# Spreading a column of token values over the free axis: a PE transpose in place of a float32 product with the identity

## The chip, the cores and the metric

The kernel runs on one core of one Trainium2 chip. The metric is the device time of one execution in microseconds, lower is better. TensorE (PE) multiplies matrices, VectorE (DVE) and ScalarE (ACT) do elementwise work, GpSimd (POOL) the small powers, and SyncE's queue (SP) issues the loads.

## The reference, cut to what matters

Two transformer-like blocks run over 256 tokens of width 1024: a first one (gated feed-forward layers, forgetting attention, a gated delta rule, cross attention to a memory) and a second of depth 2 (feed-forward layers, a convolution and a state-space mixer, a gated projection). Between the layers stands, again and again, a norm over the width of each token:

```python
def rms_norm(x, gain):
    xf = x.astype(jnp.float32)
    y = xf * lax.rsqrt(jnp.mean(xf * xf, axis=-1, keepdims=True) + EPS)
    return (y * gain.astype(jnp.float32)).astype(x.dtype)

def l2_norm(x):
    return x * lax.rsqrt(jnp.sum(x * x, axis=-1, keepdims=True) + EPS)

def swiglu(x, w_gate, w_up, w_down):
    return (jax.nn.silu(x @ w_gate) * (x @ w_up)) @ w_down
...
def first_block(...):
    f = swiglu(rms_norm(h, ffn1_pre_norm[l]), ffn1_w_gate[l], ffn1_w_up[l], ffn1_w_down[l])
    h = h + FFN_RESIDUAL_WEIGHT * rms_norm(f, ffn1_post_norm[l])
    mixed = hybrid_mixer(rms_norm(h, mix_pre_norm[l]), ...)
    h = h + rms_norm(mixed @ w_out[l], mix_post_norm[l])
    ...
```

Everything is float32.

## The kernel before

Activations lie transposed: eight tiles of 128 features (partitions) by 256 tokens (free axis). Every weight is loaded in units of up to 128x1024, split by ACT into a rounded high half `hi` (line 299) and by DVE into the remainder `lo` (line 300), and each product of weight and activation is three matmuls of 128x256 (`mm3`: high by high, high by low, low by high), all through `mm` on line 267. `raw` has four buffers, `hi` and `lo` three each, so that a new unit waits until PE is done with the one three before it. PSUM tiles are `pm` (projections) and `px` (everything else).

A norm goes like this. The squares of the tiles are added up (`acc`), and PE sums them over the partitions, with the two halves of the tokens as stationary operands and a column of ones moving: the result has the 128 tokens of a half on the partitions, one column for each half. DVE adds the epsilon (`rv`, line 419), POOL raises it to the power -0.5 (`rs`, line 421). To multiply the activations, which have the tokens on the free axis, the column must be spread: every partition must hold the whole row of token values. That is `spread`: for each half `t`, the column, repeated 128 times along the free axis by a step of zero, is the stationary operand of a product with the identity. `rstd_b` copies the result out to `rb`; `post` and the group norm of `mixer2` read it in PSUM. The `l2_norm` values of the gated delta rule go the same way (`rk` and, with the output norm, `of`), and `mixer1` spreads a copy of its column, `mrt`.

`transpose` (line 270) is PE's transpose by the same identity; the kernel uses it elsewhere, for the chunks of the two mixers and the attention weights.

The order of work on each engine is not written out: a scheduler takes the program's operations by priority and by its own estimates of when each can start and how long it takes. `high_priority(-n)` puts an operation n places later; `late` and `APART` do so for sums and spreads, so that other products stand between the two halves of a sum or of a spread and cover the way over DVE and POOL.

Of the kernel before, what the change touches and what calls it, by code (L numbers as in the profile page):

```python
# [15 lines left out]
P = 128  # L16
# [121 lines left out]
class Net:  # L138
# [285 lines left out]
    def spread(self, r, cols=(0, 1), apart=0):  # L424

        ps = self.bank()
        for t in range(2):
            j = cols[t]
            with self.tc.high_priority(-apart * t):
                self.mm(ps[:, t * P:(t + 1) * P], r[:, j:j + 1].to_broadcast([P, P]), self.ident)  # L430
        return ps[:, :S]

    def rstd_b(self, acc, n, mult=1.0):
# [1066 lines left out]
```

## Time and profile before

| | |
|---|---|
| timed runs, median of 3 | 2211.42 us (2211.13 to 2215.14) |
| the profiled execution's own time | 2205.73 us |
| its span, first to last instruction | 2203.9 us |
| PE busy | 2171.3 us, 99% |
| DVE busy | 1553.1 us, 70% |
| ACT busy | 1191.8 us, 54% |
| POOL busy | 39.8 us, 2% |
| mean granted TensorE clock | 0.996 |

Times of an instruction are from its start to its end as the profiler has them. Matmuls are pipelined: an instruction on PE lasts some 0.28 us while the next starts 0.11 us after it. What a matmul costs is therefore read from the distance of starts, not from its own duration. A float32 product stands as two instructions in the profile and as one in the scheduler's order.

### The profile page before, as it was taken

Reading aid. Unit: us, or ns where it says so; the run is one execution under the profiler, and the core shown is the slowest. Engines: PE = TensorE matmul, PEld = TensorE weight load, DVE = VectorE, ACT = ScalarE, POOL = GpSimd, SP = SyncE. Lnnn points to the kernel's source line nnn. Section 1 sums busy time; section 2 is a strip of 40 time slices with the busy share of each in tenths; the row PEclk is TensorE's granted clock in tenths of the full one; section 3 lists DMA queues with packets and bytes.
Section 4 is the critical chain, followed back from the end, with each engine's and each line's share of the span. In section 5 each row is a group of like instructions: output and inputs, shape, how many; then the busy total and the mean of one; then the engine's idle time right before and its main releaser. Section 6 shows DMA issues by size and latency. Waiting matters only on the chain.

```text
span 2203.9 us, 45488 instructions
## 1 busy us (share of the span) xinstructions
PE 2171.3 (99%) x18672; PEld 2129.2 (97%) x18672; DVE 1553.1 (70%) x2608; ACT 1191.8 (54%) x2037; POOL 39.8 (2%) x54
## 2 busy tenths in 40 slices
PE   8999999999999999999999999999999999999998
PEld 8999998999999999998999999999999999999997
DVE  7756874757666766798676766676669876777666
ACT  6545635546555454676465554555456755645444
POOL 0000000000000000000000000000000000000000
PEclk9999999999999999999999999999999999999999
DMA  7565521435666566562555666656665346566663
GB/s 259 180 187 167 167 77 39 144 125 171 192 193 186 191 192 190 183 194 73 191 178 183 192 193 189 212 163 194 192 191 183 122 141 192 170 197 188 195 190 119
DMA packets 110369, 379.44 MB, mean 172 GB/s; under 512 B 12368, under 2 KB 17104, under 8 KB 110160
## 3 DMA queue, kind: packets, MB, share of 16 engines
q1 hardware_dynamic: 110160, 376.53, 54.3%
q8 instruction: 146, 2.39, 0.4%
q14 instruction: 63, 0.52, 0.1%
HBM read 375.43 MB, written 1.05 MB: 171 GB/s over the span
## 4 chain that ended last, share of the span: by engine, by line
PE 76%; DVE 2%; ACT 1%; DMA 0%; POOL 0%; issue 0%; DVEq 0%; ACTq 0%; POOLq 0%
PE pm L267 69%; PE px L267 7%; PE px L270 0%; POOL rs L421 0%; DVE lo L300 0%; ACT hi L299 0%; DMA raw<-in_ple_w_gate_dram 0%; ACT d L264 0%; DMA raw<-in_ffn_wu_dram 0%; DVE s L255 0%; DVE r L261 0%; DVE s L261 0%; DVE acc L258 0%; ACT L264 0%; DVE rb L439 0%
## 5 line engine op out<-in xcount | busy, mean ns | idle before, releaser
L267 PE MATMUL pm<-r,hi 128*128 128x256 f32 x10640 | 1845.7, 278 | 10.3 <-ACT hi L299 5.6
L267 PEld LDWEIGHTS pm<-r,hi 128*128 128x128 f32 x10640 | 1613.8, 188 | 12.9 <-ACT hi L299 10.5
L267 PE MATMUL pm<-r,lo 128*128 128x256 f32 x5320 | 1477.2, 278 | 0.9 <-DVE lo L300 0.9
L300 DVE TENSOR_TENSOR lo<-raw,hi 128x1024 fp32r<-128x1024 f32 (+1 forms) x718 | 860.8, 1200 | 476.8 <-ACT hi L299 473.0
L299 ACT CAST hi<-raw 128x1024 fp32r<-128x1024 f32 (+1 forms) x718 | 739.8, 1031 | 723.3 <-PE pm L267 580.6
L267 PEld LDWEIGHTS pm<-r,lo 128*128 128x128 f32 x5320 | 1000.3, 188 | 1.5 <-DVE lo L300 1.1
L278 ACT CAST r<-w 128x256 fp32r<-128x256 f32 x136 | 54.4, 402 | 63.9 <-DVE w L255 63.6
L255 DVE TENSOR_TENSOR t<-pm,rb 128x512 f32<-128x512 f32 (+1 forms) x132 | 78.5, 635 | 0.2
L264 ACT ACTIVATE r<-s,vec 128x256 fp32r<-128x256 f32 x136 | 65.3, 504 | 20.7 <-DVE s L261 18.1
L264 ACT ACTIVATE sq<-s 128x256 f32<-128x256 f32 x152 | 60.3, 411 | 25.0 <-DVE s L255 17.4
L261 DVE SCALAR_TENSOR_TENSOR s<-pm,vec,s 128x255 f32<-128x255 f32 x144 | 68.7, 477 | 2.3
L261 DVE SCALAR_TENSOR_TENSOR r<-s,vec,r 128x256 fp32r<-128x256 f32 x136 | 65.2, 499 | 6.0 <-ACT r L264 5.5
L267 PE MATMUL px<-r,hi 128*128 128x256 f32 x384 | 66.7, 278 | 0.0
L279 DVE TENSOR_TENSOR r<-w,r 128x256 fp32r<-128x256 f32 x136 | 57.1, 422 | 8.8 <-ACT r L278 0.4
L267 PEld LDWEIGHTS px<-r,hi 128*128 128x128 f32 x384 | 57.8, 188 | 0.0
L267 PE MATMUL px<-r,lo 128*128 128x256 f32 x192 | 53.0, 276 | 0.0
L255 DVE TENSOR_TENSOR w<-w,t 128x256 f32<-128x256 f32 x132 | 49.8, 419 | 0.5 <-ACT w L264 0.5
L264 ACT ACTIVATE w<-t 128x256 f32<-128x256 f32 x132 | 47.6, 407 | 1.3 <-DVE t L255 1.3
L421 POOL TENSOR_TENSOR rs<-rv,mhalf 128x2 f32<-128x2 f32 x26 | 19.7, 758 | 1493.3 <-DVE rv L419 1493.3
L258 DVE TENSOR_TENSOR acc<-acc,sq 128x256 f32<-128x256 f32 x94 | 39.5, 421 | 5.8 <-ACT sq L264 2.6
L267 PE MATMUL px<-d,d 128*64 128x128 f32 (+2 forms) x384 | 42.7, 291 | 0.3 <-DVE d L255 0.2
L255 DVE TENSOR_TENSOR s<-s,px 128x256 f32<-128x256 f32 x82 | 30.1, 416 | 15.0 <-PE px L267 15.0
(232 smaller groups left out, 1368.1 us busy)
## 6 DMA issues: line engine op xcount, KB each, us to landing
raw<-in_w_in_dram SPq DMA_DIRECT2D x188, 512.0 KB, 4.3
raw<-in_ffn_wg_dram SPq DMA_DIRECT2D x88, 512.0 KB, 4.5
raw<-in_ffn_wu_dram SPq DMA_DIRECT2D x88, 512.0 KB, 4.5
raw<-in_ffn_wd_dram SPq DMA_DIRECT2D x80, 512.0 KB, 4.1
raw<-in_ffn_w_up_dram SPq DMA_DIRECT2D x44, 512.0 KB, 4.6
raw<-in_ffn_w_gate_dram SPq DMA_DIRECT2D x43, 512.0 KB, 4.5
raw<-in_ffn_w_down_dram SPq DMA_DIRECT2D x40, 512.0 KB, 3.9
raw<-in_m_w_out_dram SPq DMA_DIRECT2D x32, 512.0 KB, 4.0
```

The costliest lines, as they stand in the source:

```text
L255: self.nc.vector.tensor_tensor(out=out, in0=a, in1=b, op=ALU.mult)
L258: self.nc.vector.tensor_tensor(out=out, in0=a, in1=b, op=ALU.add)
L261: self.nc.vector.scalar_tensor_tensor(out=out, in0=a, scalar=s, in1=b, op0=op0, op1=op1)
L264: self.nc.scalar.activation(out, a, f, **kw)
L267: self.nc.tensor.matmul(out, lhsT=lhsT, rhs=rhs, start=start, stop=stop)
L278: nc.scalar.copy(hi, src)
L279: nc.vector.tensor_tensor(out=lo, in0=src, in1=hi, op=ALU.subtract)
L299: nc.scalar.copy(o, r)
L300: nc.vector.tensor_tensor(out=d, in0=r, in1=o, op=ALU.subtract)
L421: self.nc.gpsimd.tensor_tensor(out=r, in0=v, in1=self.mhalf[:, :2], op=ALU.pow)
```

## The change

In `spread` the product of the repeated column with the identity becomes a transpose of the repeated column. The value at (m, n) is the column's entry n either way.

```diff
         for t in range(2):
             j = cols[t]
             with self.tc.high_priority(-apart * t):
-                self.mm(ps[:, t * P:(t + 1) * P], r[:, j:j + 1].to_broadcast([P, P]), self.ident)
+                self.transpose(ps[:, t * P:(t + 1) * P], r[:, j:j + 1].to_broadcast([P, P]))
         return ps[:, :S]
```

```python
    def transpose(self, out, a, k=P):
        self.nc.tensor.transpose(out, a, self.ident[:k, :k])
```

The scheduler orders the changed program anew. On PE most places keep their order; the two openings of `ffn` near 533 and 723 us don't. This is PE at the first of them, before (`acc` is the sum of squares, `rs` the column, `r` an activation tile with its two halves, `hi` and `lo` the weights):

```order
L267 MATMUL px<-ones_134,acc_196 128x1
L267 MATMUL pm<-r_108,hi 128x256
L267 MATMUL pm<-r_108,lo 128x256
L267 MATMUL pm<-r_106,lo 128x256
L267 MATMUL px<-ones_134,acc_196 128x1
L267 MATMUL pm<-r_107,hi 128x256 x2
L267 MATMUL pm<-r_107,lo 128x256
L267 MATMUL pm<-r_108,hi 128x256 x2
L267 MATMUL pm<-r_108,lo 128x256
L267 MATMUL pm<-r_105,hi 128x256 x2
L267 MATMUL px<-con,rs_242 128x128
```

Eight products stand between the second half of the sum and the first half of the spread. The same place on PE after the change:

```order
L267 MATMUL px<-ones_134,acc_196 128x1
L267 MATMUL pm<-r_108,lo 128x256
L267 MATMUL px<-ones_134,acc_196 128x1
L267 MATMUL pm<-r_108,hi 128x256
L267 MATMUL pm<-r_108,lo 128x256
L267 MATMUL pm<-r_107,hi 128x256 x2
L270 MATMUL px<-con,rs_242 128x128
```

Four products stand there now; the sum's second half has moved ten places back in PE's order, the first half of the spread six, the second half none.

The other place is the end of `mixer1`, near 400 us, where the four gated heads are scaled by the spread `of` and split into `r_119` to `r_122` for the product with `w_out`. ACT there, before:

```order
L771 COPY d_2665<-pm 128x256
L278 CAST r_119<-s_93 128x256
L278 CAST r_120<-s_94 128x256
L278 CAST r_121<-s_95 128x256
L278 CAST r_122<-s_96 128x256
L299 CAST hi<-raw 128x1024
L264 ACTIVATE sq_191<-pm 128x256
```

And ACT after the change:

```order
L771 COPY d_2665<-pm 128x256
L278 CAST r_119<-s_93 128x256
L278 CAST r_120<-s_94 128x256
L278 CAST r_121<-s_95 128x256
L299 CAST hi<-raw 128x1024
L278 CAST r_122<-s_96 128x256
L264 ACTIVATE sq_191<-pm 128x256
```

The rounding of a weight unit has moved ahead of the last head's cast. On DVE the low half of `r_122` stands behind that unit's low half in the same way.

## Rows read from the trace of the kernel before

**Rows 1.** The page: PE's busy us, share and instructions, then the chain's shares.

```profile
PE 2171.3 (99%) x18672; PEld 2129.2 (97%) x18672; DVE 1553.1 (70%) x2608; ACT 1191.8 (54%) x2037; POOL 39.8 (2%) x54
...
PE 76%; DVE 2%; ACT 1%; DMA 0%; POOL 0%; issue 0%; DVEq 0%; ACTq 0%; POOLq 0%
```

**Rows 2.** The waits: engine line <- releaser: us in total, times, longest us.

```profile
ACT hi L299 <- PE pm L267: 580.6, 393, 4.0
...
PE px L267 <- POOL rs L421: 7.9, 11, 1.4
...
PE px L267 <- POOL rk L683: 1.0, 1, 1.0
PE px L267 <- DVE of L255: 1.0, 1, 1.0
...
PE px L267 <- DVE mrt L628: 0.4, 1, 0.4
```

**Rows 3.** Groups on PE by shape: busy us, mean ns of one, idle before.

```profile
L267 PE MATMUL px<-con,rs 128*128 128x128 f32 x100 | 20.2, 295 | 7.9 <-POOL rs L421 7.9
...
L270 PE MATMUL px<-con,s 128*128 128x128 f32 x80 | 11.5, 273 | 0.0
...
L267 PE MATMUL px<-con,rk 128*128 128x128 f32 x16 | 2.1, 281 | 1.0 <-POOL rk L683 1.0
```

**Rows 4.** PE in order of time, a spread amid products (start us, us).

```profile
203.47 0.60 PE L267 MATMUL px<-con,rs 128*128 128x128 f32 x4
203.83 0.36 PE L267 MATMUL pm<-r,lo 128*128 128x256 f32 x1
204.03 0.40 PE L267 MATMUL pm<-r,hi 128*128 128x256 f32 x2
```

**Rows 5.** PE in order of time, two transposes amid products.

```profile
347.38 0.38 PE L270 MATMUL pm<-con,fp 128*128 128x128 f32 x2
347.52 0.48 PE L267 MATMUL pm<-r,hi 128*128 128x256 f32 x2
347.83 0.28 PE L267 MATMUL pm<-r,lo 128*128 128x256 f32 x1
```

**Rows 6.** PE in order of time, transposes in a row in `mixer2`.

```profile
1004.06 1.15 PE L270 MATMUL px<-con,s 128*128 128x128 f32 x9
```

**Rows 7.** PE in order of time, behind an idle: a spread, then transposes.

```profile
58.04 0.71 PE L267 MATMUL px<-con,rs 128*128 128x128 f32 x4 [1.39 <-POOL rs L421]
58.51 0.48 PE L267 MATMUL pm<-r,hi 128*128 128x256 f32 x2
...
462.81 0.63 PE L270 MATMUL px<-con,d 128*128 128x128 f32 x4 [0.19 <-DVE d L1040]
463.27 0.81 PE L267 MATMUL px<-s,s 128*128 128x256 f32 x3
```

**Rows 8.** DVE in order of time, behind a spread at 905 us.

```profile
905.90 0.42 DVE L439 COPY rb<-px 128x256 f32<-128x256 f32 x1 [0.98 <-PE px L267]
```

**Rows 9.** PE and POOL in order of time, `ffn` opening: sum, spread, power.

```profile
531.82 0.28 PE L267 MATMUL px<-ones,acc 128*128 128x1 f32 x2
...
533.18 0.49 PE L267 MATMUL px<-con,rs 128*128 128x128 f32 x2
...
532.43 0.70 POOL L421 TENSOR_TENSOR rs<-rv,mhalf 128x2 f32<-128x2 f32 x1 [15.99 <-DVE rv L419]
```

**Rows 10.** PE and ACT in order of time, behind the `of` spreads.

```profile
403.76 0.40 PE L267 MATMUL pm<-r,hi 128*128 128x256 f32 x2
...
402.41 1.07 ACT L278 CAST r<-s 128x256 fp32r<-128x256 f32 x3 [1.40 <-DVE s L255]
403.84 1.05 ACT L299 CAST hi<-raw 128x1024 fp32r<-128x1024 f32 x1 [0.37 <-PE pm L267]
```

**Rows 11.** Stretches: us, busy of PE, PEld, DVE, ACT, POOL, then PEclk, DMA.

```profile
360.70:364.10 3.40, 3.40 (x14) 2.46 (x13) 0.00 (x0) 1.61 (x5) 0.00 (x0) 0.50 0.33 119
...
377.80:381.20 3.40, 3.40 (x17) 3.18 (x15) 1.33 (x4) 1.42 (x4) 0.00 (x0) 0.50 0.38 139
```

## The prediction, made before the changed kernel had run

> **What bounds the kernel now.** I read the page first: TensorE is busy for 2171.3 us of a span of 2203.9, 99% [rows 1], and the chain that ended last runs through PE for 76% with no other engine above 2% [rows 1]. DVE (70%) and ACT (54%) have room. Then the waits [rows 2]: ACT, which rounds each weight tile to its high half, idles 580.6 us because PE has not yet freed a buffer. So the weight stream is paced by PE and not PE by the stream, and time taken off PE anywhere should reach the end. PE itself hardly waits; but 11 of its waits, 7.9 us together, are for the GpSimd power that makes `rs`, the very column that is spread next, and one each for `rk`, `of` and `mrt`, the other three columns that are spread. Last I read the spreads themselves, by shape [rows 3] and in order of time [rows 4 to 7].
>
> **What the change removes and adds.** `spread` runs 34 times: 25 times on `rs` (six `ffn`, one `mem_attn`, two `mixer2` and two `ple` through `rstd_b`; four `post`; one `mem_pre`; eight group norms; one at the end), four on `rk`, four on `of`, one on `mrt`. Each is two 128x128 float32 products. The hardware runs a float32 product as two matmul instructions: 25 spreads are 50 products and stand as x100, the four `rk` spreads as x16 [rows 3]. The transposes that the kernel has already stand as one each (the 80 of type `con,s` as x80) [rows 3]. So 136 PE instructions become 68, each with its weight load.
>
> The price of one spread before, amid other work: from 203.47 to 204.03 run its four passes and one ordinary product, 0.56 us [rows 4]. An ordinary product takes 0.12 (2171.3 us over 18672 instructions [rows 1]), so the spread costs 0.44 us, 0.11 a pass. The price after, from the kernel's own transposes between ordinary products: from 347.38 to 347.83 run two transposes and two products, 0.45 us [rows 5]; less 0.23 that is 0.22 us for two. Nine transposes in a row agree: 1.15 us less the tail of the last, 0.27, over eight steps is 0.11 each [rows 6]. One spread saves 0.44 - 0.22 = 0.22 us, and 34 save **7.5 us**. PE has no slack here that hides work, so all of it lies on the path; where PE idles behind a spread, DVE waits for that spread's last pass (0.98 us of DVE idle ended by it at 905.90 [rows 8]) and starts as much earlier.
>
> Here a rule speaks for more. The table in "TensorE: Matmul & The Clock Gate" (the Trainium skill, section Terms) calls the transpose mode four times faster for FP32; by it a spread would fall from 0.44 to 0.11 us. The trace does not bear that out: 0.11 us is what one transpose takes, and a spread needs two [rows 6].
>
> **Behind an idle.** A spread that starts after a wait pays more: its four passes take 0.47 us at 58.04 against 0.36 at 203.47 (to the start of the next product), 0.11 more [rows 4, 7]. Four transposes after a wait take 0.46 us at 462.81, against four of 0.11, so 0.02 to 0.03 more [rows 7]. That is 0.08 us further gain for each of the 14 spreads that PE waited for (11 + 1 + 1 + 1 [rows 2]): **1.1 us**. No transpose of a broadcast column stands in the trace, so the bounds are 0 and 0.11 x 14 = 1.5; I take 1.1, from the nearest row.
>
> **What moves.** The scheduler places work by its own estimates, and a shorter spread shifts them. Nearly every spread keeps its neighbours: the number of products between the last sum and the spread is the same in 32 of 34 places. Two differ, the openings of `ffn` at 533 and 723 us. There eight products stood between the second half of the last sum and the spread, and four stand there now. The chain sum, DVE `rv`, POOL `rs`, spread took from 531.82 to 533.18 with `rs` ready at 532.43 + 0.70 = 533.13 [rows 9]: eight products just covered it. Without four of them PE idles 4 x 0.12 = 0.47 us, twice: **-0.9 us**. The bounds are 0 (if the sum's input is there earlier) and 1.2 each (the sum itself stands ten products later, all of them lost).
>
> The third place is after the `of` spreads. ACT's cast of `r_122`, the last gated head, now stands behind the rounding of a weight tile that started only at 403.84, when PE freed its buffer [rows 10], and DVE's low half of it behind that tile's low half. PE frees that buffer some 0.96 us earlier (eight passes, 0.88, and 0.08 behind the idle), so the cast of `r_122` ends near 402.9 + 1.05 + 0.4 = 404.3 (1.05 for the tile, some 0.4 for a head's cast, three of which took 1.07 [rows 10]). PE uses the high half of `r_122` twelve products after `r_119`, which it reached at 403.76 [rows 10] and now reaches near 402.8, so near 404.2; the low half is as close. I charge **-0.3 us**; the bounds are 0 and 1.2 (if the buffer is freed no earlier). On DVE other weight halves move by a place or two with more room than that, and on SP one weight load passes one `memT` load at the start, where neither is waited for: nothing.
>
> Sum: 7.5 + 1.1 - 0.9 - 0.3 = **7.4 us** off the profiled execution's 2205.73 (span 2203.9 and 1.8 around it). That execution lies 5.7 us under the median of the timed runs, 2211.42; I assume the same distance after, hence **2211.4 - 7.4 = 2204.0 us**.
>
> **The clock.** In two stretches of 3.4 us, at 360.7 and 377.8, PE was granted 0.50 of its clock, 1.2 instead of 2.4 GHz [rows 11], in the stage of small gated-delta matmuls. Each costs at most half its length, 1.7 us. The change shifts that stage by some 2 us and could add or remove one: +-1.7 us in the range.
>
> **Rivals.**
> (a) The moved places cost their upper bounds: 2 x 1.2 + 1.2 instead of 1.2 in all. Gain 5.0, time 2206.4. For it: at these places the low halves reach PE with little to spare. Against it: PE-paced buffers come free earlier. Chance 0.11.
> (b) The waits swallow the gain: if what PE waits for at the 14 idles comes at a time that PE does not set, each idle grows by what was saved before it, and only the last spread's 0.3 us is left: 2211.1. Against it: the wait for `rs` begins with a sum on PE [rows 9], and ACT waits for PE, not the reverse [rows 2]. Chance 0.09.
> (c) It does not do what it says: a transpose of a column repeated with step zero runs as two passes like the product, 2211.4, or with the moved waits 2212.6. Against it: the one instruction per transpose, in every shape here [rows 3]. Chance 0.04.
> (d) The slower side: a run of transposes behind an idle drops the granted clock. At each of the 14 spreads after a wait PE would then run 3.4 us at half rate, 1.7 us: 14 x 1.7 - 7.4 = 16.4 slower, 2227.8. It decides from five places on (8.5 us against 7.4), and from seven the loss is over 0.2%. Against it: nine transposes in a row ran at 0.11 us each [rows 6], and both drops here stand elsewhere [rows 11]. The rule it rests on stands in "TensorE: Matmul & The Clock Gate" (the Trainium skill, Part 4: PE-mode transpose), which says that a transpose does not count as activity for the clock, and gives some 275 ns for one in a kernel; the trace has a mean of 273 ns from start to end of one [rows 3], yet 0.11 us from one to the next. Chance 0.04.
> (e) A transpose costs a quarter of the product, 0.11 us a spread: 34 x 0.33 = 11.2, plus 1.1, less 1.2, 2200.3. Against it [rows 6]. Chance 0.02.
>
> **How the numbers follow.** The forecast keeps 0.70. Its own range is 2204.0 with one clock drop more or less (1.7) and the unknown ends (+1 and -1.5): 2201 to 2207. I widen the low end to 2200.3, which takes in (e); the top of 2207 takes in (a). That leaves out (b), (c), (d) and the tail of the forecast, some 0.2. Faster by over 0.2% (4.4 us, about what a measurement here can tell from no change) means under 2207.0: nearly all of the forecast (0.68), most of (a) (0.09) and (e): 0.79. Within 0.2%: (b), (c) and the rests: 0.17. Slower: (d), 0.04.
>
> **What would show it.** PE should have 68 matmuls fewer, and each spread two of line 270, 0.11 us apart. PE's busy time should fall by some 7.5 us. At the two `ffn` openings PE's wait for `rs` should be about 0.5 us where it now hardly waits. After `of`, a wait for `r_122` of some tenths. If PE's busy time falls and its idle time grows by as much, (b) was right; if line 270 shows two instructions for each, (c); if more than two stretches at 0.50 stand in the profile, and right behind spreads, (d).

## The result, and the profile after

The changed kernel takes **2241.97 us** (median of 5 runs, 2233.31 to 2245.76); the kernel before, beside it, 2215.14 (5 runs, 2211.13 to 2219.52). The ratio is 1.0114, interval [1.0086, 1.0143]: 1.1% slower, where 0.3% faster was forecast. The profiled execution took 2233.31 us with a span of 2231.5, 27.6 longer than before.

The page's first row (busy us, share of the span, instructions by engine) and groups on PE by shape (busy us, mean ns of one, idle before), after:

```profile
PE 2197.7 (98%) x18604; PEld 2154.9 (97%) x18604; DVE 1556.9 (70%) x2608; ACT 1190.3 (53%) x2037; POOL 39.7 (2%) x54
```

```profile
L267 PE MATMUL pm<-r,hi 128*128 128x256 f32 x10640 | 1877.7, 281 | 10.6 <-ACT hi L299 5.8 <-DVE w L255 2.1 <-DVE s L255 2.1
L267 PE MATMUL pm<-r,lo 128*128 128x256 f32 x5320 | 1490.3, 280 | 0.6 <-DVE lo L300 0.6
...
L270 PE MATMUL px<-con,rs 128*128 128x128 f32 x50 | 13.6, 293 | 8.9 <-POOL rs L421 8.9
...
L270 PE MATMUL px<-con,rk 128*128 128x128 f32 x8 | 1.1, 279 | 1.0 <-POOL rk L683 1.0
```

Against [rows 1] PE has 68 instructions fewer and is busy 26.4 us **longer**; its idle time hardly moved. Against [rows 3] the spreads halved as counted, 100 to 50 and 16 to 8. So the loss sits in PE work that nobody edited. The first two groups name it; the same two of the kernel before read:

```profile
L267 PE MATMUL pm<-r,hi 128*128 128x256 f32 x10640 | 1845.7, 278 | 10.3 <-ACT hi L299 5.6 <-DVE s L255 2.1 <-DVE w L255 2.1
L267 PE MATMUL pm<-r,lo 128*128 128x256 f32 x5320 | 1477.2, 278 | 0.9 <-DVE lo L300 0.9
```

The same 10,640 and 5,320 ordinary products (a weight tile with the 256 tokens, 128x256) last 281 and 280 ns where they lasted 278. Where? A stretch view over five long stretches without any wait (us, PE busy and its instructions, granted clock, DMA share, GB/s), before and then the same five after:

```profile
58.71:199.93 141.22, 141.22 (x1202) 1.00 0.59 183
727.07:900.48 173.41, 173.41 (x1533) 1.00 0.62 192
1260.54:1431.12 170.58, 170.58 (x1508) 1.00 0.64 197
1466.89:1640.31 173.42, 173.42 (x1533) 1.00 0.63 192
2000.37:2172.88 172.51, 172.51 (x1525) 1.00 0.62 192
```

```profile
59.90:195.79 135.89, 135.89 (x1201) 1.00 0.62 190
719.55:899.75 180.20, 180.20 (x1532) 1.00 0.61 187
1264.13:1441.38 177.25, 177.25 (x1507) 1.00 0.62 190
1476.42:1656.62 180.20, 180.20 (x1533) 1.00 0.60 186
2021.53:2200.79 179.26, 179.26 (x1525) 1.00 0.60 185
```

These stretches show two paces and nothing between: 173.41 / 1533 = 0.1131 us a product, or 180.20 / 1532 = 0.1176, at a granted clock of 1.00 in both. (From start to start, without the products that a window cuts at its ends, it is 113.3 and 117.8 ns.) Each of them keeps its pace from its first product to its last. The first stretch went from the long pace to the short one (141.22 to 135.89), the other four the other way, 6.7 or 6.8 us each. I counted the steps, from one ordinary product to the next, in both profiled executions; a stretch of at least nine steps counts as long where their mean is 116.5 ns or more: **2,641 of 16,594 steps stood at the long pace before, 10,310 of 16,589 after**. That is 7,669 x 4.5 ns = 34.5 us; less the forecast gain of 7.4 it leaves 27.1, against 27.6 measured.

### The profile page after: what moved, and what is told of

The parts are those of the page before. It is cut to its first block, busy times and chain, and to the rows that moved or that the text cites. A ratio compares the mean times of both kernels' runs of the same rounds, so it can differ in the third digit from the quotient of the medians.

```text
span 2231.5 us, 45347 instructions
## 1 busy us (share of the span) xinstructions
PE 2197.7 (98%) x18604; PEld 2154.9 (97%) x18604; DVE 1556.9 (70%) x2608; ACT 1190.3 (53%) x2037; POOL 39.7 (2%) x54
## 4 chain that ended last, share of the span: by engine, by line
PE 77%; DVE 1%; ACT 1%; POOL 0%; issue 0%; DVEq 0%; ACTq 0%; POOLq 0%
PE pm L267 70%; PE px L267 6%; PE px L270 1%; POOL rs L421 0%; DVE lo L300 0%; ACT hi L299 0%; ACT d L264 0%; DVE s L255 0%; DVE s L261 0%; DVE r L261 0%; DVE acc L258 0%; ACT L264 0%; DVE rb L439 0%; DVE w L255 0%; DVE rv L419 0%
## 5 line engine op out<-in xcount | busy, mean ns | idle before, releaser
L267 PE MATMUL pm<-r,hi 128*128 128x256 f32 x10640 | 1877.7, 281 | 10.6 <-ACT hi L299 5.8
L264 ACT ACTIVATE sq<-s 128x256 f32<-128x256 f32 x152 | 60.1, 410 | 24.8 <-DVE s L255 17.4
```

Of the source, the lines that this page charges most:

```text
L264: self.nc.scalar.activation(out, a, f, **kw)
L267: self.nc.tensor.matmul(out, lhsT=lhsT, rhs=rhs, start=start, stop=stop)
```

## What sets the pace: experiments

The switch itself: PE in order of time (start us, us) at the last spread ahead of the second of those stretches, before:

```profile
726.61 0.28 PE L267 MATMUL px<-r,lo 128*128 128x256 f32 x1
726.73 0.38 PE L267 MATMUL px<-con,rs 128*128 128x128 f32 x2
726.87 0.48 PE L267 MATMUL px<-r,hi 128*128 128x256 f32 x2
727.19 0.28 PE L267 MATMUL px<-r,lo 128*128 128x256 f32 x1
727.30 0.39 PE L267 MATMUL px<-r,hi 128*128 128x256 f32 x2
```

and after:

```profile
718.87 0.28 PE L267 MATMUL px<-r,lo 128*128 128x256 f32 x1
718.98 0.39 PE L267 MATMUL px<-r,hi 128*128 128x256 f32 x2
719.21 0.28 PE L267 MATMUL px<-r,lo 128*128 128x256 f32 x1
719.32 0.27 PE L270 MATMUL px<-con,rs 128*128 128x128 f32 x1
719.35 0.48 PE L267 MATMUL px<-r,hi 128*128 128x256 f32 x2
719.67 0.28 PE L267 MATMUL px<-r,lo 128*128 128x256 f32 x1
719.78 0.40 PE L267 MATMUL px<-r,hi 128*128 128x256 f32 x2
720.02 0.28 PE L267 MATMUL px<-r,lo 128*128 128x256 f32 x1
```

Nobody waits at either place. From one `r,lo` to the next, three products, it is 0.34 us ahead of the lone transpose (718.87 to 719.21) and 0.35 behind it (719.67 to 720.02), and so it stays for 1,530 products. The three products with the transpose in them (719.21 to 719.67) take 0.46 us, so the transpose itself costs 0.12; the two passes before cost 0.23 (726.61 to 727.19, less 0.34).

Of the 10,310 long steps after, 8,012 stand right behind such a lone transpose in the running stream. First theory, "count": one PE instruction between ordinary products leaves the long pace, two leave the short one. Rivals: "kind" (a transpose does it, in any number) and "places" (the moved instructions, or chance). Below, a number of long steps is always that of a run's one profiled execution, and the time the median of all its executions.

**Each transpose issued twice.**

```diff
                 self.transpose(ps[:, t * P:(t + 1) * P], r[:, j:j + 1].to_broadcast([P, P]))
+                self.transpose(ps[:, t * P:(t + 1) * P], r[:, j:j + 1].to_broadcast([P, P]))
```

> Each transpose of the spreads is issued twice, writing the same values to the same place, so that a half of a spread is two PE instructions, as it was with the product, and the places of the change are kept. Count theory: what matters is how many PE instructions stand between ordinary 128x256 products; one leaves them 0.118 us apart afterwards, two leave them 0.113 apart. Then the long stretches of products run at 0.113 again and the kernel is at the time of before, 2212 to 2217 us, 27 us faster than the changed kernel with 68 instructions more. Kind theory: a transpose, however many, leaves the products at 0.118: 2242 + 68 x 0.11 = 2249 us. Places theory (the loss comes from the two openings of ffn and the other moved instructions, or from chance): 2242 to 2249 us.

Measured: 2226.23 us, 1.0079 [1.0056, 1.0102]. With 68 transposes more it is 15 us above the kernel before that ran beside it, where the changed kernel was 27 above: less than half of the 27 us that count expected to come back, and the intervals of the two ratios overlap. 6,945 steps stood at the long pace. Two of its stretches, either of which took 173.4 us before:

```profile
725.50:905.58 180.08, 180.08 (x1532) 1.00 0.61 185
1478.16:1651.46 173.30, 173.30 (x1532) 1.00 0.63 192
```

Its order explains what is missing: at most second halves the scheduler put an ordinary product between the two copies, so they were lone again.

**The two halves of a spread back to back; and the product put back where the halves stand apart.**

```diff
-            with self.tc.high_priority(-apart * t):
+            with self.tc.high_priority(5 * t):
```

> The changed kernel, with the second transpose of each spread put directly behind the first one; in the changed kernel 2 to 30 ordinary products stand between the two halves of 25 spreads. Count theory: two instructions together leave the products at 0.113 us, and the spread keeps its saving: 2215 - 7.5 = 2207 us, with 1 to 2 us either way because the second half now comes earlier on PE. Kind theory and places theory: as the changed kernel, 2240 us or so.

```diff
-                self.transpose(ps[:, t * P:(t + 1) * P], r[:, j:j + 1].to_broadcast([P, P]))
+                if apart:
+                    self.mm(ps[:, t * P:(t + 1) * P], r[:, j:j + 1].to_broadcast([P, P]), self.ident)
+                else:
+                    self.transpose(ps[:, t * P:(t + 1) * P], r[:, j:j + 1].to_broadcast([P, P]))
```

> The float32 product is put back where the two halves of a spread stand apart among ordinary products (19 spreads: ffn, mem_attn, mixer2, ple, group norms); the transpose stays where the halves stand together (15 spreads). The order of instructions is that of the changed kernel, the openings of ffn included. Count theory and kind theory alike: stretches at 0.113 us, 15 x 0.22 = 3.3 us less than before, less 0.9 for the openings: 2212 to 2215 us. Places theory: the order of the changed kernel costs what it costs, 2235 to 2242 us.

Measured: back to back 2209.00 us, 0.9993 [0.9963, 1.0024], 7,720 long steps in an execution of 2216.45 us (its executions run from 2189.93 to 2217.39); mixed 2206.80, 0.9990 [0.9963, 1.0018], 1,698 long steps. Mixed settles "places": it has the changed kernel's order, and the loss is gone. Back to back has the time that count expected, but not its reason: many of its pairs stand right behind an idle of PE, where the pace begins anew, and pairs in the stream mostly kept the pace that they met, so that three stretches of over 1,500 steps ran at the long one.

**Which half comes last.** The first half a transpose and the second a product, and the reverse (`if apart and t == 1`, `if apart and t == 0` in place of `if apart`).

> At the 19 spreads whose halves stand apart, the first half is a transpose and the second half the float32 product; the other 15 spreads are transposes. Last-interruption theory (a pace is set where an interruption of the stream ends: the two passes of a product leave 0.113 us a step whatever ran before, a lone transpose leaves 0.118 when the stream came at 0.113): the long stretches follow the second half, so they run at 0.113, and only the 2 to 30 products between the halves may be slow. Time as mixed less 19 x 0.11 = 2.1: about 2205 us. If instead the number of transposes in the program or the first half decides, the time lies near 2240.

> The mirror image: at the same 19 spreads the first half is the product and the second half the transpose. PE has the same number of instructions of each kind as with the halves the other way round, in the same places. Last-interruption theory: the first half leaves the stream at 0.113 and the lone transpose behind it turns it to 0.118 at all of the long stretches, so it is at least as slow as the changed kernel, 2240 to 2260 us (all 16,600 steps at 0.118 instead of the 2,600 slow ones of before would be 62 us). Any theory that counts instructions or transposes alone: as the other way round, about 2205.

Measured: transpose first 2217.83 us, 1.0046 [1.0026, 1.0066]; transpose last 2233.34, 1.0117 [1.0085, 1.0149]. The same instructions in the same places differ by 15 us, so the order of the two kinds matters. But transpose first is 13 us above what I expected, with 6,512 long steps, and transpose last 7 us under the expected 2240 to 2260. The last-interruption theory has fallen: a product does not bring back the short pace, it **keeps** the pace that the stream had, and the lone transpose ahead of it had already turned it.

**Four extra products to bring the short pace back.** The transpose-first kernel with one unread product each behind the `mem_pre` spread and behind the transposes of the three small projections.

> The kernel with the transpose in the first half and the product in the second half of the 19 spreads, and four more float32 products whose results nobody reads, each placed some products behind an idle of PE where a long stretch begins by chance at either pace: one behind the spread of mem_pre (1199 products follow) and one behind the transposes of each of the three small projections (558 products follow two of them). Last-interruption theory: these stretches run at 0.113 as well, which saves 5.3 us and twice 2.5 us where they were slow, for 4 x 0.22 us of products: 2 to 6 us less on average than without, about 2201 us, and a smaller scatter between executions. If the pace behind an idle cannot be set in this way: 2206 us, the price of the four products more.

Measured: 2216.94 us, 1.0036 [1.0015, 1.0058], 6,011 long steps: no gain, as a product that keeps the pace would have it. A miss for the theory it was made for.

**One transpose more, two transposes more**, to the kernel before, behind the product of each second half that stands apart:

```diff
                 self.mm(ps[:, t * P:(t + 1) * P], r[:, j:j + 1].to_broadcast([P, P]), self.ident)
+                for i in range(1 if apart and t else 0):
+                    with self.tc.high_priority(5 * i + 5):
+                        self.transpose(ps[:, t * P:(t + 1) * P], r[:, j:j + 1].to_broadcast([P, P]))
```

> The kernel before, untouched, plus one transpose that writes the same values again, directly behind the product of the second half of the 19 spreads whose halves stand apart: three PE instructions there, 19 x 0.11 = 2.1 us of work more. Theory so far (a product of two passes keeps the pace that the stream came with, a lone transpose turns 0.113 into 0.118): the stretches behind these spreads turn to 0.118, 8,000 to 13,000 slow steps, 2235 to 2255 us. If three instructions count as one interruption that keeps the pace: 2207 + 2 = 2209 us.

> The kernel before plus two transposes, back to back, directly behind the same 19 products: four PE instructions there, 4.2 us of work more. Theory: an even number of instructions keeps the pace as the product alone does, under 4,000 slow steps, 2207 + 4 = 2211 us: two transposes more are faster by some 30 us than one more. If a transpose of any number turns the pace: as with one more, and 2 us on top.

Measured: one more 2212.52 us, 0.9989 [0.9964, 1.0014], 2,297 long steps; two more 2219.41, 1.0018 [0.9996, 1.0040], 2,275. (Two more is 7 us above one more, for 2 us of passes; its executions were granted 0.992 to 0.995 of the clock, those of one more 0.994 to 0.997.) Odd against even is not it: behind a product, one transpose more keeps the pace as none and two do. Among these, what turns the pace is a transpose **standing alone**, in either direction. The table counts, over the traces of the kernels told of so far in which both paces occur, and of the one that follows next, what stretches did at an interruption without idle (a pace read from the last three steps ahead and the last four of the stretch behind):

| between ordinary products | short stays short | short turns long | long stays long | long turns short |
|---|---|---|---|---|
| a product, two passes | 71 | 0 | 11 | 5 |
| a product and one transpose | 10 | 0 | 0 | 3 |
| a product and two transposes | 9 | 0 | 0 | 4 |
| two transposes | 23 | 1 | 3 | 7 |
| four transposes | 5 | 0 | 4 | 15 |
| **one transpose** | **0** | **32** | 3 | 12 |
| transpose, ordinary product, transpose | 0 | 15 | 1 | 3 |
| **two products together, four passes** | **0** | **4** | 2 | 0 |

(The row of four transposes is mostly the kernel's own in `mixer2`, not spreads.) The last row keeps this from being a rule on lone passes: where both halves of a spread stand together as products, in the kernel before and in the two with transposes added to it, four passes without idle turned the short pace as well, four times of four. This is one of them, before; three products take 0.34 us ahead of it (426.89 to 427.23) and 0.36 behind it (428.02 to 428.38):

```profile
426.89 0.28 PE L267 MATMUL pm<-r,lo 128*128 128x256 f32 x1
427.01 0.39 PE L267 MATMUL pm<-r,hi 128*128 128x256 f32 x2
427.23 0.28 PE L267 MATMUL pm<-r,lo 128*128 128x256 f32 x1
427.35 0.28 PE L267 MATMUL pm<-r,hi 128*128 128x256 f32 x1
427.46 0.60 PE L267 MATMUL px<-con,rs 128*128 128x128 f32 x4
427.82 0.36 PE L267 MATMUL pm<-r,hi 128*128 128x256 f32 x1
428.02 0.28 PE L267 MATMUL pm<-r,lo 128*128 128x256 f32 x1
428.14 0.40 PE L267 MATMUL pm<-r,hi 128*128 128x256 f32 x2
428.38 0.28 PE L267 MATMUL pm<-r,lo 128*128 128x256 f32 x1
```

So do the sums of squares (`ones,sq`, one column moving) in the same traces: twelve passes in a row turned the short pace in 21 cases of 21. So neither the number of passes nor their kind is the rule by itself.

**Pairs in the running stream.** The changed kernel with both transposes back to back where the second one stood, behind more products:

```diff
-            with self.tc.high_priority(-apart * t):
+            with self.tc.high_priority(20 * t - apart):
```

> The changed kernel with both transposes of a spread back to back at the place where the second one stood, some products behind the last sum, so that no lone transpose stands between ordinary products and fewer of the pairs stand behind an idle. Lone theory (one PE instruction alone between ordinary products turns 0.113 into 0.118, two or more keep the pace that was there): the long stretches run as in the kernel before, 2,000 to 4,000 slow steps, and the saving of the transposes is kept, 7.5 us, with up to 4 us of idle less: 2200 to 2205 us against some 2211 of the kernel before. If a pair turns the pace as well: over 6,000 slow steps, 2215 to 2240.

Measured: **2194.63 us, 0.9926 [0.9898, 0.9953]**, faster than both kernels and under the expected 2200 to 2205, with 3,192 long steps (one stretch of 1,545 behind a short idle among them). PE at a pair, and PE's wait for the power (us in total, times, longest):

```profile
1256.14 0.39 PE L267 MATMUL pm<-r,hi 128*128 128x256 f32 x2
1256.37 0.28 PE L267 MATMUL pm<-r,lo 128*128 128x256 f32 x1
1256.48 0.38 PE L270 MATMUL px<-con,rs 128*128 128x128 f32 x2
1256.62 0.48 PE L267 MATMUL px<-r,hi 128*128 128x256 f32 x2
```

```profile
PE px L270 <- POOL rs L421: 2.5, 2, 1.4
```

The stretch behind that pair runs at 113.3 ns. The wait was 7.9 us in 11 places before [rows 2]; the later place saves 5.4 us and the transposes 7.5, some 13 of the 16 us; the rest stays open.

**A bfloat16 product in place of the transpose**, the same count of another kind, twice: with 8 bytes per partition for the two rounded columns, and with 64. (The identity in bfloat16 that it needs is also made earlier.)

```diff
+        q = self.t("half16", [P, 2], BF16)
+        self.nc.vector.tensor_copy(q, r[:, cols[0]:cols[0] + 2])
...
-                self.transpose(ps[:, t * P:(t + 1) * P], r[:, j:j + 1].to_broadcast([P, P]))
+                self.mm(ps[:, t * P:(t + 1) * P], q[:, t:t + 1].to_broadcast([P, P]), self.identb)
```

> A half of a spread is one instruction, but not a transpose: a bfloat16 product of the repeated column with a bfloat16 identity. The column is rounded to bfloat16 by one DVE copy per spread first, so the spread values are rounded, and the output with them. Count theory: one instruction alone leaves the products at 0.118 us, so the long stretches are slow, 2242 us plus up to 34 x 0.2 for the copies, 2242 to 2249. Kind theory: no transpose is there, so the stretches run at 0.113 and the time is 2207 plus the copies, 2207 to 2215.

> The bfloat16 product again in place of each transpose (spread values rounded to bfloat16), but its two small tiles now take 64 bytes of a partition in all and not 8, so that the operands of the ordinary products behind them start at multiples of 64 bytes again. Address theory: the flat 0.120 us a step of the first such kernel came from the 8 bytes, and here the steps are 0.113 or 0.118. Then: count theory, a lone instruction of another kind leaves 0.118 too, over 8,000 slow steps, 2235 to 2250 us; kind theory, only a transpose does, under 4,000 slow steps, 2207 to 2215 us. If the steps are 0.120 again, the address theory falls and the time is 2290.

Measured: 2290.53 and 2287.43 us, 1.0366 and 1.0361. They don't tell count from kind, since every stretch of both runs at a third pace, 120.0 ns, even ahead of the first spread. My address theory for the first, that 8 bytes had broken a multiple of 64, fell with the second. What both share is that the activation tiles moved. So I moved tiles without any bfloat16 product.

**Unused bytes ahead of the activation tiles**, in the kernel before and in the changed one: 64, then 32. (Small working tiles of the same pool may have moved with them.)

```diff
+        self.sc.tile([P, 16], F32, tag="gap", name="gap", bufs=1)
         ap = pool("arena", 1)
```

> The kernel before with 64 unused bytes per partition put ahead of the tiles of the token values and their rounded halves, and nothing else: their addresses become multiples of 128 bytes, where they are 64 past one. Address theory: all steps at a flat 0.120 us as in the bfloat16 kernel, where the same tiles had moved by 64 bytes, and no stretch at 0.113 or 0.118: 2211 + 16,600 x 0.006 = some 2290 us. If the bfloat16 products caused the flat pace: 2207.

> The changed kernel with the same 64 unused bytes. If every step then takes 0.120 us whatever interrupts the stream, the change can no longer turn the pace, and what is left is its own work: the 7.5 us of PE passes and what was counted at the idles, 6 to 9 us less than the kernel before with the same 64 bytes, some 2283 us. If the loss of the change has another cause than the pace, it stays, 20 to 30 us more than the kernel before with the 64 bytes.

> The kernel before with 32 unused bytes ahead of the tiles of the token values and their halves, whose addresses become 96 past a multiple of 128 bytes (64 past one before, 0 with 64 unused bytes). Address theory in the narrow form (0.120 flat at multiples of 128 alone): steps at 0.113 and 0.118 as before, 2207 to 2216 us. In the wide form (only 64 past a multiple has the fast paces): 0.120 flat, 2290 to 2300.

> The changed kernel with the same 32 unused bytes. If the paces are flat there, the change shows its own work alone, 6 to 9 us less than the kernel before with 32 bytes. If both paces are there, it loses 20 to 30 us to it, as without the bytes.

| unused bytes | before | changed | difference | pace |
|---|---|---|---|---|
| 64 | 2299.57 (2296.19 to 2302.88) | 2292.03 (2291.84 to 2296.86) | **-7.5** | 120.0 ns, all stretches |
| 32 | 2275.67 (2272.23 to 2276.03) | 2267.03 (2265.06 to 2267.77) | **-8.6** | 118.3 ns, nearly all |

With 64 bytes the stretch behind the same spread reads as follows in the kernel before, 183.59 / 1532 = 0.1198 us a product:

```profile
746.22:929.81 183.59, 183.59 (x1532) 1.00 0.58 182
```

and in the changed kernel, the same:

```profile
744.38:927.96 183.58, 183.58 (x1532) 1.00 0.58 184
```

The page's first row, before and then changed, with 64 bytes:

```profile
PE 2265.2 (99%) x18672; PEld 2223.3 (97%) x18672; DVE 1559.3 (68%) x2608; ACT 1188.3 (52%) x2037; POOL 39.8 (2%) x54
```

```profile
PE 2258.8 (99%) x18604; PEld 2216.4 (97%) x18604; DVE 1559.4 (68%) x2608; ACT 1188.3 (52%) x2037; POOL 39.6 (2%) x54
```

PE is busy 6.4 us less for the change, where it was 26.4 more without the bytes. This is the test of the whole account. Where the tiles lie such that the pace does not turn, the change is worth -7.5 and -8.6 us; the forecast was -7.4. Each is a difference of two medians of four to six executions that scatter by 3 to 7 us, so the match is no closer than that. Of the two forms of the address theory neither held in full: at 32 bytes the two paces are gone, but the flat one is 118.3 and not 120.0.

## Why the prediction was wrong

**The step that failed** is the one that was no step: "An ordinary product takes 0.12 (2171.3 us over 18672 instructions [rows 1])". That mean hides two paces, 0.1131 and 0.1176, and the sum left the 16,600 ordinary steps untouched by an edit of 68. The long pace stood in the trace of before, in the stretch that begins right behind a spread that I quoted: 58.71 to 199.93, 141.22 us for 1202 instructions, against 173.41 for 1533 behind 727. The same count divided into two stretches would have shown it. No rival had this either; the slower one, (d), put the loss on the granted clock, at 0.04. What the runs showed in its place: 7,669 more ordinary steps than before stood at 117.8 ns instead of 113.3, for 34.5 us, most of them behind lone transposes (8,012 of the 10,310 long steps).

**What held.**
- *68 instructions fewer, one for each half:* 18672 to 18604; (c) is out.
- *0.44 to 0.22 us a spread, more behind an idle:* behind the idle at 58 us the spread took 0.47 us to the next product [rows 7]. After, it took 0.19 (59.50 to 59.69), a saving of 0.28 where 0.22 + 0.08 was taken. (The 0.08 came from a mixed reading: 0.47 and 0.36 run to the start of the next product, while the 0.44 that transposes were held against is four whole steps.)

```profile
59.50 0.43 PE L270 MATMUL px<-con,rs 128*128 128x128 f32 x2 [1.38 <-POOL rs L421]
59.69 0.49 PE L267 MATMUL pm<-r,hi 128*128 128x256 f32 x2
```

- *The two `ffn` openings, 0.47 us each:* 0.52 and 0.51, and POOL's power at the first one begins at 525.89 where it began at 532.43 [rows 9]. At this point the changed kernel was 6.5 us **ahead**, 5.3 of it from the first stretch's turn to the short pace, which is luck as far as the runs show: that stretch begins behind an idle, and behind the same two transposes and the same idle of 1.38 us it ran at 117.8 ns in the kernel with the transpose first. From there to the end the changed kernel lost 34.

```profile
526.64 0.32 PE L270 MATMUL px<-con,rs 128*128 128x128 f32 x1 [0.52 <-POOL rs L421]
...
716.99 0.32 PE L270 MATMUL px<-con,rs 128*128 128x128 f32 x1 [0.51 <-POOL rs L421]
```

```profile
525.89 0.70 POOL L421 TENSOR_TENSOR rs<-rv,mhalf 128x2 f32<-128x2 f32 x1 [16.88 <-DVE rv L419]
```

- *`r_122` behind the weight rounding, 0.3 us:* the cast came where it was put and ended at 398.49, and PE's product began at 398.55; DVE's low half ended at 399.79, and its product began at 399.84. From 398.35 to 399.01 and from 399.46 to 400.07 PE makes four steps each in 0.66 and 0.61 us, where four of 0.1176 are 0.47: 0.33 late in all.
- *The sum, -7.4:* -7.5 and -8.6 where the pace is flat.

**The other rivals.** (a) The moved places cost 0.5, 0.5 and 0.3, not their bounds of 1.2. (b) The waits did not swallow the gain: PE's wait for `rs` went from 7.9 us in 11 places to 8.9 in 13, the two openings. (e) is out with the spread behind the idle; "TensorE: Matmul & The Clock Gate" (the Trainium skill, Terms), which calls the transpose mode four times faster for FP32, is not borne out by these rows either. (d) Two stretches near the gated-delta products again fell to half clock, here (355.0 to 358.4 and 372.0 to 375.4) as before [rows 11], and none behind a spread; a third, which the prediction did not count, lies at the very end of both, from 2193.6 and 2222.1, where PE mostly waits. In the kernel with four extra products one did begin behind the transposes of `mem_pre`, 0.50 from 60.1 to 63.5: one place, at most 1.7 us.

Not every long step after is due to a lone transpose: two stretches of 558 stand behind a short idle and the transposes of the small projections. That the pace behind an idle falls differently between executions of one kernel, too, and that this makes the scatter of the kernel before (2200.76 to 2220.05 in one comparison, against 3 to 7 us with unused bytes), is argued from one trace of each kernel and not shown.

## What to carry to other kernels

Before an edit of a few instructions is priced, divide the span of several long stretches of the untouched stream by their instructions: if they disagree, the stream has paces, and an edit that interrupts it can cost more than its own work. Here a single transpose standing alone between weight products did that, and so did four product passes together; one product or a pair of transposes kept the short pace in 94 cases of 95, and pairs placed where PE need not wait gave the fastest kernel of this case. That is found for this layout of tiles; another stream has to be looked at anew. And to test a small gain on its own, run it and its base where the paces are flat.

## What was not expected of the hardware

A stream of weight load and 128x256 product ran, with the same instructions at the same granted clock of 1.00, at 113.3, 117.8, 118.3 or 120.0 ns a step: the first two by what had interrupted it, the others with unused bytes ahead of the activation tiles. 64 unused bytes per partition cost the kernel before 3.8% (1.0381 [1.0346, 1.0417]), 32 cost 2.8% (1.0279 [1.0247, 1.0312]). In the stretch behind the spread at 727 and 719 us the weight loads for the high halves, mean ns of one, before and after:

```profile
L267 PEld LDWEIGHTS pm<-r,hi 128*128 128x128 f32 x968 | 145.5, 188 | 0.0
```

```profile
L267 PEld LDWEIGHTS pm<-r,hi 128*128 128x128 f32 x968 | 148.5, 190 | 0.0
```

One load in three lasts longer at the long pace, and with 64 bytes all do. This looks as if the weight loads and the moving tokens met in reading SBUF, in a phase that an interruption sets; no run here isolates that, and why one transpose or four product passes turn the pace and two passes don't stays open. "SBUF — State Buffer" (the Trainium skill, Who interferes with whom) gives PE two independent read ports and says that it never waits on anyone; whatever the mechanism, these rows show a pace of PE that changes when nothing but unused bytes ahead of the tiles is added.
